# Feed-forward pairs of a two-layer encoder kernel: the fourth weight sum's products one own unit later, its adding transfer in halves, and another adding transfer one own unit sooner

## The chip, the cores and the metric

The kernel runs on one core of a Trainium2 chip. A core has five engines with instruction queues of their own: TensorE (PE: matrix products), VectorE (DVE), ScalarE (ACT), GpSimd (POOL) and SyncE (SP), which in this kernel only starts transfers. PE reads its operands from the on-chip memory and accumulates in a small memory of eight banks. Transfers between the chip's large memory and the on-chip memory are started by SP or by POOL and then run by themselves on the core's 16 DMA engines. The metric is the device time of one execution in microseconds (us), the median of several runs.

## What is computed

A two-layer encoder over 256 rows of 2048 numbers, all float32. Cut to what matters here:

```python
def sq_relu_mlp(h, g, w1, w2):
    a = jax.nn.relu(rms_norm(h, g) @ w1)      # w1: 2048 x 8192
    return (a * a) @ w2                       # w2: 8192 x 2048

h = h + attention_a(h) @ a_w_out              # projections, gated attention
h = h + sq_relu_mlp(h, g0, w1[0], w2[0])      # first feed-forward layer
k_sh, v_sh = split(rms_norm(h) @ kv_w)
h = h + attention_b(h, k_sh, v_sh) @ b_w_out
h = h + sq_relu_mlp(h, g1, w1[1], w2[1])      # second feed-forward layer
```

The change touches the two feed-forward layers alone.

## The kernel before

**Products.** A float32 product is made of three passes. Every block of 128 x 1024 weights is split into a rounded part `hi` (ACT, line 323) and the rest `lo = w - hi` (DVE, line 324); the activations are split likewise. PE then does hi x hi (line 592), hi weights x lo activations (line 594) and lo weights x hi activations (line 596). `hi` and `lo` have three buffers each, so that the splits run at most three blocks ahead of PE, and a split waits until PE has finished with the block three places before.

**Pairs.** The feed-forward weights are worked off in 32 pairs, each two blocks of 512 output columns over all 2048 rows of the sum. 30 of them are "deep": half of a deep pair's work is done by Strassen's scheme, with seven products instead of eight. Its seven weight operands ("forms") are the four quarters `11`, `12`, `21`, `22` and the three weight sums that replace them as the pair goes on, T3 = 22 + 12, then T2 = T3 + 11, then T1 = 12 + 11, then T4 = T2 + 21. There are four sums in all, and the forms of a pair are used in the order 11, T3, T2, T1, and after that 21, T4 and 22. Each form is 128 x 2048, that is two blocks (the second marked h: T4, T4h), with six matmuls of 512 columns per block. The other half of a pair is eight "own units" of plain products, a4 to a7 and b4 to b7, with twelve matmuls each. A pair is thus 14 blocks of forms and 8 own units, 180 matmuls.

**Who makes the sums.** T3 and T2 are made by DVE (line 964), half by half. T1 and T4 are made by an *adding transfer*, started by POOL (line 974): it fetches the other quarter from the large memory and adds it in place, T1 onto the tile of quarter 12, T4 onto the tile of T2 (which is that of T3, `wT3`). An adding transfer can start only when the old content has been read.

**Order.** A plan is written out before any instruction: for every kind of pair a string gives the order of own units (a4, b4, ...) and of forms (F, the next of 21, T4, 22 in the order of the table `FO`). The kinds are `early` (first pair of a layer, not deep), `second` (the next one, deep), `ahead0` and `ahead1` (first weight matrix, later pairs), `deep0` and `deep1` (second weight matrix). After the first two pairs of a layer they alternate deep0, ahead0, deep1, ahead1, three times round, and end with deep0, deep1. The last three own units of a pair (b5, b6, b7) stand between the first four forms of the next. Tables such as `W2S` say how many own units ahead of a pair its quarters 12, 22, 21, 11 are fetched, its T3 is made, and its T1 is started (the sixth number). The splits run along that plan with up to three blocks in hand (`top_up`), and so do the fetches of own units (`raw`, `zraw`). On DVE, ACT, PE and SP the instructions stay in written order; on POOL a scheduler may move them.

**Other work beside it.** The results of the first weight matrix need a squared ReLU and a turn of the tile: DVE transposes into `z` (line 440), and for some of them 16 small transfers move `z` to `q` in one hop (line 466, half of them started by POOL, half by SP); later ACT reads `q` (line 1037, then 1042 and 1044) and DVE finishes (line 1048, sums in lines 395 to 398 and 405). Lines 936 and 299 are SP's fetches of quarters (`w`) and own units (`raw`).

Of the kernel before, what the change touches and what calls it, by code (L numbers as in the profile page):

```python
# [46 lines left out]
    "LONG": ((0, 1, 2, 5, 9, 10, 11, 14, 14), (0, 0, 0, 4, 7, 9), (0, 0, 1, 2, 5, 5), (1, 0, 1, 4, 5, 5)),  # L47
    "OFH": (11, 10, 2, 7, 7, 6),
    "OFK": (9, 9, 4, 8, 8, 4),
# [3 lines left out]
    "OSH": (10, 7, 9, 6, 5, 1),  # L53
    "OSK": (9, 7, 4, 7, 5, 1),
    "OUTH": "F a2 a3 a4 b2 a5 b3 b4 F F G G b5 a6 a7 G b6 b7 G c2 G c3 G d2 c4 c5 c6 G c7 d3 d4",
# [18 lines left out]
    "XOH": (9, 13, 12, 11),  # L74
    "XOK": (10, 14, 12, 14),
    "XS": (0, 5, 5, 0),
# [23 lines left out]
def trunk(ctx: ExitStack, tc: tile.TileContext, xT, xr, gs, hg, bf, wgate, w_in, w_oa, w1a, w1fa, w1sa, w2fa, w2sa,  # L100
# [188 lines left out]
    def load(parts=1, queue=SY, apart=None):  # L289
        src = units.popleft()  # L290
        if isinstance(src, Form):
            raws.append((src, ()))
            return
        extra[1] += 1
        raw = qkv.tile([P, UN], F32, name="zraw", tag="z", bufs=2) if extra[0] and extra[1] % 5 == 0 else wraw.tile([P, UN], F32, name="raw")
        n = UN // parts
        cuts = [slice(i * n, (i + 1) * n) for i in range(parts)]
        if apart is None:
            queue.dma_start(raw, src)
        else:  # L300
            for q, c in zip((queue, apart), cuts):
                q.dma_start(raw[:, c], src[:, c])
        raws.append((raw, cuts))

    def issue(parts=1):
        form = None
        if not raws:
            load(parts)
        raw, cuts = raws.popleft()
        if not cuts:  # L310
            form, half = raw, raw.half
            assert form.name in form.pair.has, "unit early"
            if form.name in ("T3", "T2"):
                assert form.name + str(int(half)) in form.pair.has, "unit early"
            form.pair.issued.add(form.name)
            raw, cuts = form.pair.t[form.name], [slice(0, form.pair.cols - UN if half else UN)]
            if half:
                raw = raw[:, UN:]
        n = cuts[-1].stop
        hi = wsp.tile([P, n], F32R, name="hi" if n == UN else "hih", bufs=3 if n == UN else 1)  # L320
        lo = wsp.tile([P, n], F32R, name="lo" if n == UN else "loh", bufs=3 if n == UN else 1)
        for c in cuts:
            S.activation(hi[:, c], raw[:, c], AF.Copy)  # L323
            V.tensor_tensor(lo[:, c], raw[:, c], hi[:, c].bitcast(F32), op=ALU.subtract)  # L324
        ready.append((hi, lo, n < UN))
        if form and form.pair.deep and form.name == "T3":
            make(form.pair, "T2", int(half))
        elif form and form.pair.order == "second" and form.name == "T2":
            put(form.pair, "T4", int(half))
        elif form and half == form.pair.wide:  # L330
            if form.name == "T3":
                make(form.pair, "T2")
            elif form.name == "T2" and form.pair.adds:
                put(form.pair, "T4")
# [5 lines left out]
    def top_up(ahead=AHEAD, early=EARLY):  # L340
        while (units or raws) and sum(1 for r in ready if not r[2]) <= ahead and not (half_next() and any(r[2] for r in ready)):
            issue()
        while units and sum(1 for r in raws if r[1]) < early + extra[0]:
            load()
# [593 lines left out]
    def make(p, name, half=None):  # L938
        t = p.t
        if half == 1:  # L940
            pass
        elif name == "T3":
            if p.order in ("query", ""):
                t[name] = query_room(0)
            elif p.order == "kv0":
                t[name] = query_room(3)
            elif p.order in LAZY:
                t[name] = acts.tile([P, 2 * UN], F32, name="wT3", tag="act")[:, :UN]
            else:
                t[name] = prob.tile([P, 4 * UN], F32, name="wT3", tag="p", bufs=1) if p.order == "early" else room("bias", "wT3")  # L950
        else:
            t[name] = t[{"T1": "12", "T2": "T3", "T4": "11"}[name]]
        a, b = {"T1": ("12", "11"), "T3": ("22", "12"), "T2": ("T3", "11"), "T4": ("21", "T2")}[name]
        cols = slice(0, p.cols) if half is None else slice(half * UN, min(half * UN + UN, p.cols))
        d, a, b = (t[i][:, cols] for i in (name, a, b))
        if name == "T3":
            assert {"22", "12"} <= p.has and "T1" not in p.has, "T3 order"
        if name == "T1":
            assert "T30" in p.has and "T31" in p.has, ("T1 order", p.order, p.has, p.units, getattr(p, "at", 0))
        for k in (0, 1):  # L960
            if half in (None, k):
                p.has.add(name + str(k))
        p.has.add(name)
        V.tensor_tensor(d, a, b, op=ALU.add)

    def put(p, name, half=None):

        at, other = {"T1": ("12", "11"), "T4": ("T2", "21")}[name]
        p.t[name] = p.t[at]
        if name == "T1":  # L970
            assert "T30" in p.has and "T31" in p.has, ("T1 order", p.order, p.has, p.units, getattr(p, "at", 0))
        p.has.add(name)
        cols = slice(0, p.cols) if half is None else slice(half * UN, half * UN + UN)
        G.dma_start(p.t[name][:, cols], p.big[other][:, cols], accum_op=ALU.add)
# [388 lines left out]
```

## Time and profile before

| what | value |
|---|---|
| device time, median of 3 runs | 2053.66 us (2053.36 to 2055.16) |
| span of the profiled execution, first to last instruction | 2051.8 us |
| PE busy | 2042.6 us, 100% |
| DVE, ACT, POOL busy | 87%, 68%, 12% |
| granted TensorE clock | 1.000 |
| first feed-forward layer | about 366 to 1023 us of the span |
| second feed-forward layer | about 1384 us to the end |

The page gives no time of the profiled execution other than its span; the median of the runs is 1.9 us longer. The rows of the profile read: line, engine, operation, output<-inputs, count, then busy time and mean duration, or, in a view in order of time, the start and the length in us ahead of the instruction. Idle time of the engine just before an instruction stands in square brackets with what ended it.

### The profile page before, as it was taken

What the parts mean: (1) busy time and instruction counts of PE and PEld (TensorE: products, weight loads), DVE (VectorE), ACT (ScalarE), POOL (GpSimd) and SP (SyncE); (2) the same over time, 40 slices, a digit from 0 to 9 for tenths busy, and PEclk for the clock granted to TensorE, in tenths of its full rate; (3) what the DMA queues carried; (4) which work ended last, traced back from release to release, by engine and by line L of the source; (5) the groups of instructions that cost most, each with busy time, mean ns of one, the idle gap of its engine ahead of it and who ended that gap; (6) DMA issues with size and microseconds to landing.
All of it is one profiled execution on the core that took longest, in us unless ns stands there. A gap on an engine that the chain in (4) does not pass through costs nothing.

```text
span 2051.8 us, 27095 instructions
## 1 busy us (share of the span) xinstructions
PE 2042.6 (100%) x9062; PEld 1688.9 (82%) x9062; DVE 1784.1 (87%) x2065; ACT 1404.8 (68%) x1805; POOL 244.2 (12%) x351
## 2 busy tenths in 40 slices
PE   9999999999999999999999999999999999999999
PEld 8888888878888888888878888888888888888887
DVE  7788798899898898899988788889988988988996
ACT  7766676677677676677778666667866676776764
POOL 1121010021111102101012111100111111111020
PEclk9999999999999999999999999999999999999999
DMA  8898888898888898898879888888988888988985
GB/s 321 259 293 273 272 279 245 306 268 266 296 258 285 259 297 271 248 292 273 264 242 300 278 256 285 258 264 286 286 290 267 271 262 289 264 287 261 295 260 149
DMA packets 175021, 557.78 MB, mean 272 GB/s; under 512 B 40592, under 2 KB 69152, under 8 KB 152096
## 3 DMA queue, kind: packets, MB, share of 16 engines
q1 hardware_dynamic: 153824, 464.99, 63.7%
q0 software_dynamic: 20768, 90.75, 22.5%
q8 instruction: 71, 1.16, 0.2%
q14 instruction: 70, 0.57, 0.1%
q10 hardware_dynamic: 288, 0.30, 0.1%
HBM read 516.07 MB, written 27.29 MB: 265 GB/s over the span
## 4 chain that ended last, share of the span: by engine, by line
PE 94%; DVE 3%; DMA 1%; ACT 1%; issue 1%; SPq 0%; ACTq 0%; POOL 0%; DVEq 0%; POOLq 0%
PE acc L596 22%; PE acc L592 22%; PE acc L594 22%; PE s L596 9%; PE s L592 9%; PE s L594 9%; DVE lo L324 1%; DMA raw<-in_w_in 1%; PE po L729 1%; PE po L766 1%; ACT hi L323 0%; PE po L767 0%; PE po L728 0%; DMA turn<-z 0%; DMA raw<-in_w_qb 0%
## 5 line engine op out<-in xcount | busy, mean ns | idle before, releaser
L324 DVE TENSOR_TENSOR lo<-raw,hi 128x1024 fp32r<-128x1024 f32 (+1 forms) x409 | 494.1, 1212 | 80.4 <-ACT hi L323 76.3
L323 ACT ACTIVATE hi<-raw 128x1024 fp32r<-128x1024 f32 (+1 forms) x409 | 429.7, 1054 | 192.2 <-PE acc L594 131.0
L592 PE MATMUL acc<-hi,act 128*128 128x512 f32 x1774 | 496.2, 392 | 1.2 <-ACT hi L323 1.1
L596 PE MATMUL acc<-lo,act 128*128 128x512 f32 x1774 | 491.1, 390 | 1.5 <-DVE lo L324 1.4
L594 PE MATMUL acc<-hi,act 128*128 128x512 f32 x1774 | 490.3, 389 | 0.0
L596 PEld LDWEIGHTS acc<-lo,act 128*128 128x128 f32 x1774 | 332.3, 188 | 73.2 <-DVE lo L324 4.2
L594 PEld LDWEIGHTS acc<-hi,act 128*128 128x128 f32 x1774 | 332.9, 188 | 69.7
L592 PEld LDWEIGHTS acc<-hi,act 128*128 128x128 f32 x1774 | 331.4, 188 | 69.8 <-ACT hi L323 1.9
L323 ACT ACTIVATE hi<-w 128x1024 fp32r<-128x1024 f32 x254 | 267.1, 1058 | 127.9 <-PE acc L594 85.2
L324 DVE TENSOR_TENSOR lo<-wT,hi 128x1024 fp32r<-128x1024 f32 x220 | 267.1, 1221 | 65.0 <-ACT hi L323 61.4
L324 DVE TENSOR_TENSOR lo<-w,hi 128x1024 fp32r<-128x1024 f32 x254 | 305.5, 1218 | 15.3 <-ACT hi L323 13.5
L323 ACT ACTIVATE hi<-wT 128x1024 fp32r<-128x1024 f32 x220 | 232.0, 1060 | 97.3 <-PE acc L594 46.2
L592 PE MATMUL s<-hi,act 128*128 128x512 f32 x530 | 146.3, 391 | 0.2 <-ACT hi L323 0.2
L596 PE MATMUL s<-lo,act 128*128 128x512 f32 x530 | 145.2, 389 | 0.4 <-DVE lo L324 0.3
L594 PE MATMUL s<-hi,act 128*128 128x512 f32 x530 | 144.8, 388 | 0.0
L466 POOL DMA_DIRECT2D q<-z x192 | 95.6, 511 | 251.8 <-DVE z L440 217.3
L596 PEld LDWEIGHTS s<-lo,act 128*128 128x128 f32 x530 | 99.0, 188 | 22.0 <-DVE lo L324 1.7
L594 PEld LDWEIGHTS s<-hi,act 128*128 128x128 f32 x530 | 99.3, 188 | 20.7
L592 PEld LDWEIGHTS s<-hi,act 128*128 128x128 f32 x530 | 98.9, 188 | 20.9 <-ACT hi L323 0.8
L596 PE MATMUL s<-lo,S 128*128 128x512 f32 x288 | 88.8, 389 | 0.7 <-DVE lo L324 0.7
L592 PE MATMUL s<-hi,S 128*128 128x512 f32 x288 | 89.4, 392 | 0.0
L594 PE MATMUL s<-hi,S 128*128 128x512 f32 x288 | 88.7, 389 | 0.0
(217 smaller groups left out, 2285.6 us busy)
## 6 DMA issues: line engine op xcount, KB each, us to landing
raw<-in_w_in SPq DMA_DIRECT2D x75, 512.0 KB, 5.8
w<-in_w2fa SPq DMA_DIRECT2D x32, 1024.0 KB, 6.5
w<-in_w2fb SPq DMA_DIRECT2D x32, 1024.0 KB, 6.0
w<-in_w1fa SPq DMA_DIRECT2D x28, 1024.0 KB, 6.9
w<-in_w1fb SPq DMA_DIRECT2D x28, 1024.0 KB, 7.6
raw<-in_w2sa SPq DMA_DIRECT2D x52, 512.0 KB, 7.4
raw<-in_w2sb SPq DMA_DIRECT2D x50, 512.0 KB, 6.8
raw<-in_w_kv SPq DMA_DIRECT2D x48, 512.0 KB, 5.1
```

The source lines that it names most:

```text
L323: S.activation(hi[:, c], raw[:, c], AF.Copy)
L324: V.tensor_tensor(lo[:, c], raw[:, c], hi[:, c].bitcast(F32), op=ALU.subtract)
L466: (G if i % 2 else SY).dma_start(dst[32 * j : 32 * j + 32, i * n : (i + 1) * n], z[32 * i : 32 * i + 32, j * n : (j + 1) * n])
L592: TE.matmul(ps[:, cols], xh, cut(hi, j), start=first, stop=False, **kw)
L594: TE.matmul(ps[:, cols], xl, cut(hi, j), start=False, stop=False, **kw)
L596: TE.matmul(ps[:, cols], xh, cut(lo, j), start=False, stop=last, **kw)
L729: TE.matmul(s[:, P : 3 * P], q[:, a, P:T], k[:, a], start=True, stop=True)
L766: TE.matmul(po[:, :T], v[:, 0, a * P : (a + 1) * P], pT[:, :2], start=True, stop=False)
```

## The change

Three things are changed, all in feed-forward pairs.

1. In the pairs `second`, `ahead0`, `ahead1` and `deep0` the form T4 is used one own unit later: after a5 instead of before it (in `deep0` after b4). In `second` and `ahead` pairs form 22 stays where it was; `deep1` is as before.
2. The adding transfer that makes T4 is started in two halves in every deep pair: each as soon as that half of T2 has been split. Before, only `second` did so; the other 28 deep pairs started one transfer of 1 MB after the second half of T2.
3. For the second of every two pairs of the second weight matrix (`W2S`, and `W2L` for the last one), the adding transfer of T1 is started two own units ahead of the pair instead of one.

```diff
-    "ORD": {"second": "a4 F F a5 a6 a7 F b4", "ahead1": "a4 F F a5 a6 a7 F b4", "ahead0": "F a4 F a5 a6 a7 F b4", "deep1": "a4 F b4 F a5 F a6 a7",
+    "ORD": {"second": "a4 F a5 F a6 a7 F b4", "ahead1": "a4 F a5 F a6 a7 F b4", "ahead0": "F a4 a5 F a6 a7 F b4", "deep1": "a4 F b4 F a5 F a6 a7",
...
-        "deep0": "a4 F F F b4 a5 a6 a7"},
+        "deep0": "a4 F F b4 F a5 a6 a7"},
...
-    "W2L": (6, 5, 5, 5, 3, 1),
-    "W2S": (7, 7, 4, 5, 3, 1),
+    "W2L": (6, 5, 5, 5, 3, 2),
+    "W2S": (7, 7, 4, 5, 3, 2),
...
         if form and form.pair.deep and form.name == "T3":
             make(form.pair, "T2", int(half))
-        elif form and form.pair.order == "second" and form.name == "T2":
+        elif form and form.pair.deep and form.name == "T2":
             put(form.pair, "T4", int(half))
```

What this moves, at three places. First DVE in the pair `second` of the first feed-forward layer, where form 21 ends; `wT3_3799` holds T4, `raw_3861` is own unit a5, `w21` is form 21, and the last row (line 964) makes the first half of the *next* pair's T3. Before:

```order
L324 TENSOR_TENSOR lo_4057<-w21_3753,hi_4056 128x1024
L1016 TENSOR_TENSOR s_3866<-s_3865,p7_3940 128x512
L324 TENSOR_TENSOR lo_4078<-wT3_3799,hi_4077 128x1024
L324 TENSOR_TENSOR lo_4088<-wT3_3799,hi_4087 128x1024
L405 TENSOR_TENSOR Sh_4033<-sum_4034,Sh_4033 128x512
L405 TENSOR_TENSOR Sh_4033<-sum_4035,Sh_4033 128x512
L324 TENSOR_TENSOR lo_4102<-raw_3861,hi_4101 128x1024
L324 TENSOR_TENSOR lo_4114<-zraw_3921,hi_4113 128x1024
L324 TENSOR_TENSOR lo_4126<-raw_3964,hi_4125 128x1024
L964 TENSOR_TENSOR wT3_4145<-w22_4073,w12_4003 128x1024
```

And now:

```order
L324 TENSOR_TENSOR lo_4057<-w21_3753,hi_4056 128x1024
L1016 TENSOR_TENSOR s_3866<-s_3865,p7_3940 128x512
L324 TENSOR_TENSOR lo_4078<-raw_3861,hi_4077 128x1024
L324 TENSOR_TENSOR lo_4090<-wT3_3799,hi_4089 128x1024
L405 TENSOR_TENSOR Sh_4033<-sum_4034,Sh_4033 128x512
L405 TENSOR_TENSOR Sh_4033<-sum_4035,Sh_4033 128x512
L324 TENSOR_TENSOR lo_4104<-wT3_3799,hi_4103 128x1024
L964 TENSOR_TENSOR wT3_4119<-w22_4073,w12_4003 128x1024
L324 TENSOR_TENSOR lo_4122<-zraw_3921,hi_4121 128x1024
L324 TENSOR_TENSOR lo_4134<-raw_3964,hi_4133 128x1024
```

The split of a5 takes the place that T4's first block had, and the next pair's T3 stands ahead of the splits of a6 and a7 instead of behind them. In `ahead1` and in the `deep0` pairs that an `ahead0` follows, T3 moves ahead of the same number of splits or more.

Second, POOL from pair `deep0` on: `w12_4330` and `wT3_4527` are T1 and T4 of the first `ahead0` pair, the hop of eight is that pair's `z`, and `w12_4671` is T1 of the `deep1` pair after it, whose T4 ends the piece. Before:

```order
L974 DMA w12_4330<-in_w1fa 128x2048
L974 DMA wT3_4527<-in_w1fa 128x2048
L466 DMA q_4857<-z_4856 32x256 x8
L974 DMA w12_4671<-in_w2fa 128x2048
L974 DMA wT3_4838<-in_w2fa 128x2048
```

And now:

```order
L974 DMA w12_4331<-in_w1fa 128x2048
L974 DMA wT3_4499<-in_w1fa 128x1024 x2
L466 DMA q_4859<-z_4858 32x256 x3
L974 DMA w12_4673<-in_w2fa 128x2048
L466 DMA q_4859<-z_4858 32x256 x5
L974 DMA wT3_4840<-in_w2fa 128x1024 x2
```

T4 is two transfers, and T1 of the `deep1` pair now stands in the midst of the hop. This holds in all six `ahead0` pairs.

Third, SP in the same `ahead0` pair; `raw` and `zraw` are its own units a7 to b7 and, from `in_w2sa`, the first of the next pair; `w22`, `w11`, `w21` are quarters of the next pair. Before:

```order
L936 DMA w22_4673<-in_w2fa 128x2048
L299 DMA raw_4679<-in_w1sa 128x1024
L299 DMA raw_4741<-in_w1sa 128x1024
L936 DMA w11_4776<-in_w2fa 128x2048
L299 DMA raw_4782<-in_w1sa 128x1024
L299 DMA zraw_4794<-in_w1sa 128x1024
L299 DMA raw_4806<-in_w1sa 128x1024
L936 DMA w21_4820<-in_w2fa 128x2048
L299 DMA raw_4865<-in_w2sa 128x1024
L466 DMA q_4857<-z_4856 32x256 x8
```

And now:

```order
L936 DMA w22_4675<-in_w2fa 128x2048
L299 DMA raw_4681<-in_w1sa 128x1024
L299 DMA raw_4743<-in_w1sa 128x1024
L299 DMA raw_4755<-in_w1sa 128x1024
L936 DMA w11_4780<-in_w2fa 128x2048
L936 DMA w21_4798<-in_w2fa 128x2048
L299 DMA zraw_4804<-in_w1sa 128x1024
L299 DMA raw_4816<-in_w1sa 128x1024
L299 DMA raw_4868<-in_w2sa 128x1024
L466 DMA q_4859<-z_4858 32x256 x8
```

The fetch of quarter 21 now stands ahead of the fetches of b6 and b7. Elsewhere SP's order is as before.

## The prediction

> **What bounds the kernel now.** I read the page's busy times and its chain first, then PE's busy time stage by stage, then PE in order of time where a stage loses any.
>
> ```profile
> PE 2042.6 (100%) x9062; PEld 1688.9 (82%) x9062; DVE 1784.1 (87%) x2065; ACT 1404.8 (68%) x1805; POOL 244.2 (12%) x351
> PE 94%; DVE 3%; DMA 1%; ACT 1%; issue 1%; SPq 0%; ACTq 0%; POOL 0%; DVEq 0%; POOLq 0%
> ```
>
> PE is busy all the time and holds 94% of the chain that ended last. Busy is not full speed, so I look by stage: the pair `second` of each layer (420 to 455, 1437 to 1472), and the pairs after it.
>
> ```profile
> 420.00:455.00 35.00, 33.57 (x147) 27.13 (x147) 32.81 (x40) 26.81 (x29) 5.84 (x10) 1.00 0.93 269
> 455.00:1003.00 548.00, 548.00 (x2416) 452.97 (x2415) 495.11 (x486) 378.62 (x400) 63.85 (x107) 1.00 0.88 274
> 1437.00:1472.00 35.00, 34.93 (x153) 28.29 (x152) 34.06 (x40) 27.68 (x31) 6.18 (x11) 1.00 0.93 282
> 1472.00:2040.00 568.00, 568.00 (x2505) 469.81 (x2504) 507.12 (x496) 387.62 (x403) 63.81 (x107) 1.00 0.86 268
> ```
>
> In the two long stretches PE runs 2416 matmuls in 548 us and 2505 in 568 us: 0.2268 us each in both. Three starts show that this is full speed: the own unit b6 of an `ahead0` pair, two form blocks, and b7; twelve matmuls each time take 2.72 us, 0.2267 each.
>
> ```profile
> 541.46 1.07 PE L592 MATMUL s<-hi,act 128*128 128x512 f32 x4
> ...
> 544.18 0.62 PE L592 MATMUL acc<-hi,Sh 128*128 128x512 f32 x2
> ...
> 546.90 1.07 PE L592 MATMUL s<-hi,act 128*128 128x512 f32 x4
> ```
>
> 2416 x 0.2267 is 547.7 and 2505 x 0.2267 is 567.9, so both stretches together lose some 0.4 us. Here 28 of the 30 deep pairs lie, where most of the change is: nothing is to be won there. The Trainium skill's page "Perfetto Trace Analysis" (Identifying the Most-Contended Engine) says that matmul busy time misleads and that the busy share of weight loads tells the distance from the limit. Its 82% would leave room; the trace disagrees, as the same share (453 of 548, 83%) stands in a stretch at full pace.
>
> `second` does lose time, at form 21's second block and at T4:
>
> ```profile
> 431.83 0.61 PE L594 MATMUL acc<-hi,act 128*128 128x512 f32 x2
> 433.80 0.72 PE L596 MATMUL acc<-lo,act 128*128 128x512 f32 x2 [1.35 <-DVE lo L324]
> 434.36 0.63 PE L592 MATMUL acc<-hi,act 128*128 128x512 f32 x2
> 435.53 0.74 PE L596 MATMUL acc<-lo,act 128*128 128x512 f32 x2
> 436.11 0.62 PE L592 MATMUL acc<-hi,act 128*128 128x512 f32 x2
> ...
> 1451.23 0.64 PE L592 MATMUL acc<-hi,act 128*128 128x512 f32 x2
> 1452.96 0.62 PE L592 MATMUL acc<-hi,act 128*128 128x512 f32 x2
> ```
>
> A form block is six matmuls, 1.36 us. T4's first block takes 436.11 - 434.36 = 1.75 us in the first layer and 1.73 in the second: 0.39 and 0.37 lost, 0.76 together. Block 21h loses 1.5 at 433.80 in the first layer (1.97 us where two matmuls take 0.45). What DVE does then:
>
> ```profile
> 432.53 1.22 DVE L324 TENSOR_TENSOR lo<-w,hi 128x1024 fp32r<-128x1024 f32 x1
> 433.66 0.69 DVE L1016 TENSOR_TENSOR s<-s,p 128x512 f32<-128x512 f32 x1
> 434.26 2.35 DVE L324 TENSOR_TENSOR lo<-wT,hi 128x1024 fp32r<-128x1024 f32 x2
> 436.53 1.28 DVE L405 TENSOR_TENSOR Sh<-sum,Sh 128x512 fp32r<-128x512 f32 x2
> 437.74 1.22 DVE L324 TENSOR_TENSOR lo<-raw,hi 128x1024 fp32r<-128x1024 f32 x1
> 438.87 1.22 DVE L324 TENSOR_TENSOR lo<-zraw,hi 128x1024 fp32r<-128x1024 f32 x1
> 441.14 1.22 DVE L964 TENSOR_TENSOR wT<-w,w 128x1024 f32<-128x1024 f32 x1
> ```
>
> It works without a pause, one split each 1.13 us (437.74 to 438.87). T4's first `lo` ends at about 435.45, and PE starts the `lo` pass at 435.53: DVE is late here.
>
> **T4 one own unit later, in `second`.** Now a5's split stands in that place on DVE. Its `lo` still ends at 435.45, 1.1 after PE's start there (434.36); an own unit wants it only after eight matmuls, 1.81, not after four, 0.91. The wait goes: -0.76 in the two layers. Next late could be T4h or a6. Going on in the new order with the rows' pitches (1.13 a split or sum, 1.2 for the two of line 405): T4's `lo` ends 2.3 after that start and is wanted at 3.6; T4h's at 4.7, wanted at 5.0; the next pair's T3 ends at 5.9, a6's `lo` at 7.0, wanted at 7.25. Margins of 0.2 to 0.3, thin but above nothing. Wrong by half a microsecond, each gives up to 0.3 back per layer; so this part lies between -0.8 and +0.6, and I take -0.7, since the pitches are rows of the same stretch. Block 21h's wait stands ahead of everything that moves, and I leave it.
>
> **T4 later, in the other pairs.** PE waits for nothing there; the cover is the three blocks in hand. ACT does wait for T4's arrival (us, times, the longest):
>
> ```profile
> ACT hi L323 <- DMA wT<-in_w1fa: 6.5, 5, 2.6
> ```
>
> The longest, 2.6, is less than the 2.72 us of an own unit, so these waits go; worth 0 to PE, which doesn't feel them. What it costs: the next pair's T3 moves forward on DVE, in `deep0` to just behind T4h's split, and it needs quarter 22, fetched by SP. In one `deep0`, with PE's start on T4 (where b4 will now start):
>
> ```profile
> 638.93 0.99 SPq L936 DMA_DIRECT2D w<-in_w1fa  x2
> ...
> 642.12 0.62 PE L592 MATMUL acc<-hi,act 128*128 128x512 f32 x2
> ...
> 649.40 1.22 DVE L964 TENSOR_TENSOR wT<-w,w 128x1024 f32<-128x1024 f32 x1
> DMA to landing us min/median/max: 4.7/6.7/10.2
> ```
>
> T4h's buffer comes free at 642.12; a `hi` (1.06) and a `lo` (1.22) on, T3 could start at 644.4 instead of 649.40. The fetch of 22 starts at 638.93: 5.5 us for what takes 4.7 at least and 6.7 in the middle, so DVE may wait 1 us. a5's `lo`, next behind, ends two pitches after T3's start, at 646.7 without a wait, and is wanted 5.44 + 1.81 after 642.12, at 649.4. Cover 2.7: at the median I take 0, at the slowest it costs 10.2 - 5.5 - 2.7 = 2.0 a place, at six places.
>
> **Halves.** 28 more transfers on POOL, 0.9 us each, 25 us beside 244 busy of 2052: hidden by POOL's idle time. Landing, first of the halves in `second`, then of all adding transfers of this layer:
>
> ```profile
> DMA to landing us min/median/max: 9.9/10.8/11.7
> DMA to landing us min/median/max: 7.8/9.9/12.9
> ```
>
> The second half starts when the whole did and lands at worst 11.7 - 7.8 = 3.9 us later, at best sooner, as half is ahead of it; against 2.72 us more of time. I take 0. The Trainium skill's page "DMA: Bandwidth & Descriptors" (Anatomy of one DMA) speaks against halves: each transfer has some 2.0 us of fixed cost. By it the second half would come at most 2 us later, the sum would stay -0.7, and the hop behind it is what could suffer; no run here shows the fixed cost alone.
>
> **T1 sooner, and SP's order.** T1 had been started after the hop of `ahead0`, now it goes in after three of eight, so five hop transfers queue behind 1 MB. Rows of the hop and T1 (534.51), ACT's first use of the hop (543.73) and its next split, then an `ahead1`, where T1 already leads the hop:
>
> ```profile
> 529.22 3.97 POOL L466 DMA_DIRECT2D q<-z  x8 [23.75 <-DVE z L440]
> 534.51 0.93 POOL L974 DMA_DIRECT2D w<-in_w2fa  x1 [1.32 <-DMA q<-z]
> ...
> 543.73 1.05 ACT L1037 ACTIVATE q<-q 128x1024 f32<-128x1024 f32 x1
> 544.68 1.04 ACT L323 ACTIVATE hi<-raw 128x1024 fp32r<-128x1024 f32 x1
> ...
> 608.41 0.86 POOL L974 DMA_DIRECT2D w<-in_w2fa  x1 [20.95 <-DVE wT L964]
> 610.84 3.49 POOL L466 DMA_DIRECT2D q<-z  x7 [1.56 <-DVE z L440]
> DMA to landing us min/median/max: 8.3/8.3/8.3
> DMA to landing us min/median/max: 2.8/5.5/6.4
> ```
>
> There T1 lands at 616.7 and the hop's first at 610.84 + 6.4 = 617.2: in order behind it, the rest within 2 us. In `ahead0` T1 would start behind three hop transfers of 0.5, at about 530.8, and land at 539.1 by that row, 543.7 by the slowest of the layer; the hop's rest 1.5 us on, 540.6 to 545.2, against 543.73. The split after it starts at 544.68, and PE wants that block at 546.9 (b7's start above): 1.17 us of cover behind its 1.05. So 0 by the nearest row, and at most 0.3 by the slowest, times six places: 1.8. On SP the fetches of b6 and b7 now stand behind that of quarter 21, which can't start before its room is free (526.78):
>
> ```profile
> 526.78 0.33 SPq L936 DMA_DIRECT2D w<-in_w2fa  x1
> 538.03 1.06 ACT L323 ACTIVATE hi<-zraw 128x1024 fp32r<-128x1024 f32 x1 [1.21 <-PE s L594]
> ```
>
> b6 is split at 538.03; fetched from 527.2 it lands by 537.4 even if it takes the 10.2 us of the slowest quarter. Cost 0, but it puts 1 MB more traffic beside T1 just then, which is why I keep the slowest landing as an end.
>
> **Sum.** -0.7 in `second`, 0 elsewhere: span 2051.8 - 0.7 = 2051.1. The median of the runs is 1.9 above the span, so 2053.66 - 0.7 = 2053.0. A change of 0.2%, 4.1 us, is what a measurement of this kernel tells from none.
>
> **Rivals.** (1) The wait only moves: T4h and a6 in `second` take it over as above, +0.6 at most: 2053.7 to 2054.3. For it: margins of 0.2. (2) Slower: the hop of `ahead0` comes late behind T1. Its place is ACT at line 1037, in six pairs. It begins to cost when T1 takes over 12.6 us (530.8 + 12.6 + 1.5 = 543.73 + 1.17), and decides when it takes 13.4: 0.8 us lost six times, 4.8 less 0.7. At 14.5 it is 1.9 x 6 - 0.7 = 10.7: 2064.4. Against it: 8.3 and a maximum of 12.9. (3) T3 of `deep0` and `ahead1` waits for quarter 22: at 10.2 us 2.0 x 6 - 0.7, 2065; against it the median, 6.7. (4) Faster: 21h's wait goes too, if DVE comes there earlier: -0.7 - 1.5, 2051.4; nothing on DVE ahead of it moves. More than 4.1 us isn't there to be won.
>
> **Chances.** The forecast 0.58; (1) 0.20; (2) 0.12, two thirds of it past 4.1 us; (3) 0.06, two thirds likewise; (4) 0.04. Slower by over 0.2%: 0.08 + 0.04 and 0.02 for what I don't see, 0.14; faster 0.02; within 0.84. The range goes from all of `second`'s waits gone (2051.4, less 0.2 for the runs' own spread) to (2) and (3) at less than 4.1 us: 2051.2 to 2057.0.
>
> **What would show it.** Right: in `second` T4's first block lasts 1.36 us, 21h still waits in the first layer, and PE's two long stretches keep 0.2267 us a matmul. ACT's waits for `wT` from `in_w1fa` shrink. Wrong: idle time of ACT at line 1037 that a hop ends, DVE's line 964 waiting for a quarter, or a wait at a6 or T4h of `second`.

## The result, and the profile after

The changed kernel takes 2061.2 us, the median of six runs (2058.6 to 2065.7); the kernel before took 2055.75, the median of six too, the three shown ahead among them (2053.4 to 2057.4). Beside the experiments below its median was 2055.9 to 2056.4, so the 2053.66 from which the forecast started lay some 2 us low. The ratio is 1.0024, with a 95% interval of 1.0014 to 1.0034: slower by 0.24%, some 5 us. The forecast was 2053.0, with a range that ended at 2057.0.

The profiled execution has a span of 2059.8 us, 8.0 more than that of before. Runs of one kernel lie up to 10 us apart here, so single places are read from the traces, and what an edit is worth from the medians. The page of the changed kernel, busy times and the chain that ended last:

```profile
PE 2046.7 (99%) x9062; PEld 1686.7 (82%) x9062; DVE 1784.0 (87%) x2065; ACT 1408.2 (68%) x1805; POOL 271.5 (13%) x379
PE 88%; DMA 6%; DVE 3%; ACT 1%; issue 1%; SPq 1%; ACTq 0%; DVEq 0%; POOLq 0%
```

PE's share of the chain fell from 94% to 88%, and transfers hold 6% of it instead of 1%. POOL has 28 instructions and 27 us more, as the halves were costed. PE's busy time by stage:

```profile
420.00:455.00 35.00, 33.63 (x147) 26.98 (x146) 32.77 (x40) 26.72 (x29) 5.76 (x10) 1.00 0.95 283
455.00:1003.00 548.00, 547.74 (x2408) 450.88 (x2407) 492.87 (x483) 378.10 (x398) 76.80 (x121) 1.00 0.89 273
1437.00:1475.00 38.00, 35.30 (x152) 27.80 (x151) 33.11 (x39) 26.92 (x30) 7.26 (x12) 1.00 0.88 254
1475.00:2046.00 571.00, 570.33 (x2507) 469.32 (x2506) 508.97 (x497) 390.62 (x405) 76.70 (x121) 1.00 0.87 268
```

The first long stretch holds 2408 matmuls where it held 2416, 8 x 0.2267 = 1.8 us. The second layer's `second` needs 38 us for 152 matmuls (35 for 153 before), and the last stretch 571 us for 2507, that is 2.7 us above 0.2267 each (0.1 before). For the place of it I add up, from the starts of PE's matmuls, what each pair takes beyond 0.2267 us a matmul:

| us lost by PE | before | after |
|---|---|---|
| layer 1: `second` and first `deep0` | 2.6 | 3.4 |
| layer 1: three `ahead0` and the pairs behind them | 0.0 | 0.9 |
| layer 2: `early` (in front of all that is moved in this layer) | 0.0 | 1.2 |
| layer 2: `second` and first `deep0` | 0.9 | 5.5 |
| layer 2: three `ahead0` and the pairs behind them | 0.0 | 1.4 |

That is 8.9 more; the rest of the execution came out 0.9 shorter. Of what the change moves, two kinds of place lose. The first is the `ahead0` pair. ACT and PE in order of time, at the rows that stood at 543.73 and 546.90 before:

```profile
543.15 1.05 ACT L323 ACTIVATE hi<-wT 128x1024 fp32r<-128x1024 f32 x1
545.35 1.06 ACT L1037 ACTIVATE q<-q 128x1024 f32<-128x1024 f32 x1 [1.14 <-DMA q<-z]
546.32 1.04 ACT L323 ACTIVATE hi<-raw 128x1024 fp32r<-128x1024 f32 x1
...
545.91 0.61 PE L592 MATMUL acc<-hi,Sh 128*128 128x512 f32 x2
547.41 1.19 PE L592 MATMUL s<-hi,act 128*128 128x512 f32 x4
550.51 0.69 PE L592 MATMUL acc<-hi,Sh 128*128 128x512 f32 x2
```

ACT waits 1.14 us for the hop, b7's split behind it ends at 547.36, and PE starts b7 at 547.41. The block before b7 lasts 1.50 us instead of 1.36, and from b7's start to the next block's it is 3.10 instead of 2.72. All six `ahead0` pairs have such a wait at line 1037: 1.14, 0.45, 0.84, 0.65, 1.21 and 1.22 us. The second kind is DVE in `second`; here the second layer:

```profile
1455.49 2.36 DVE L324 TENSOR_TENSOR lo<-wT,hi 128x1024 fp32r<-128x1024 f32 x2
1460.42 1.23 DVE L964 TENSOR_TENSOR wT<-w,w 128x1024 f32<-128x1024 f32 x1 [2.57 <-issue]
1461.56 2.35 DVE L324 TENSOR_TENSOR lo<-raw,hi 128x1024 fp32r<-128x1024 f32 x2
...
1457.21 0.62 PE L592 MATMUL acc<-hi,act 128*128 128x512 f32 x2
1458.57 0.62 PE L592 MATMUL acc<-hi,act 128*128 128x512 f32 x2
1462.84 1.19 PE L596 MATMUL acc<-lo,act 128*128 128x512 f32 x4 [0.93 <-DVE lo L324]
1472.05 1.21 PE L596 MATMUL s<-lo,act 128*128 128x512 f32 x4 [0.76 <-DVE lo L324]
```

T4's first block lasts 1458.57 - 1457.21 = 1.36 us: its wait is gone, as forecast. But DVE stands still for 2.57 us ahead of the next pair's T3. That T3 needs quarter 22, which was started at 1454.51 and landed at 1460.34, 0.08 ahead of it. a6's split is queued behind T3, and PE loses 1.2 us at a6 and 1.05 at b4.

### The profile page after: what moved, and what is told of

Read it like the earlier page. It is cut to its first block, busy times and chain, and to the rows that moved or that the text cites. A ratio compares the mean times of both kernels' runs of the same rounds, so it can differ in the third digit from the quotient of the medians.

```text
span 2059.8 us, 27140 instructions
## 1 busy us (share of the span) xinstructions
PE 2046.7 (99%) x9062; PEld 1686.7 (82%) x9062; DVE 1784.0 (87%) x2065; ACT 1408.2 (68%) x1805; POOL 271.5 (13%) x379
## 4 chain that ended last, share of the span: by engine, by line
PE 88%; DMA 6%; DVE 3%; ACT 1%; issue 1%; SPq 1%; ACTq 0%; DVEq 0%; POOLq 0%
PE acc L596 20%; PE acc L592 20%; PE acc L594 20%; PE s L596 8%; PE s L592 8%; PE s L594 8%; DVE lo L324 1%; DMA q<-turn 1%; DMA raw<-in_w2sb 1%; DMA q<-z 1%; PE po L729 1%; PE po L766 1%; ACT hi L323 1%; DMA w<-in_w1fb 1%; DMA w<-in_w2fa 0%
```

## The experiments

Four theories stood against each other. **H**: the hop of `ahead0` comes late. **Q**: T3 was moved ahead of its quarter 22. **D**, formed after the first four runs: from `second` to the first `deep0` DVE works without pause, so a wait taken from T4 comes back further on. **V**: a part is only a difference between executions of any kernel. Times and ratios to the kernel before, run beside each:

| kernel | median us (runs) | ratio, 95% interval |
|---|---|---|
| `only_t1` | 2056.64 (11) | 1.0002 [0.9992, 1.0012] |
| `only_order` | 2059.93 (11) | 1.0010 [1.0000, 1.0021] |
| `only_halves` | 2055.52 (11) | 0.9997 [0.9987, 1.0007] |
| `order_halves` | 2058.01 (11) | 1.0007 [0.9997, 1.0016] |
| `ahead0_and_t1` | 2058.62 (11) | 1.0016 [1.0007, 1.0024] |
| `after_old_ahead0` | 2055.45 (11) | 1.0001 [0.9992, 1.0010] |
| `after_21_later` | 2057.18 (11) | 1.0006 [0.9997, 1.0015] |
| `order_22_sooner` | 2061.34 (8) | 1.0024 [1.0013, 1.0034] |
| `order_sums_pool` | 2075.13 (5) | 1.0096 [1.0082, 1.0110] |
| `order_lighter_dve` | 2064.40 (4) | 1.0036 [1.0022, 1.0050] |
| `second_only` | 2057.40 (10) | 1.0003 [0.9994, 1.0012] |
| `deep0_only` | 2057.83 (10) | 1.0005 [0.9996, 1.0015] |
| `second_drop` | 2054.36 (10) | 0.9991 [0.9982, 1.0001] |

### The three edits one by one

`only_t1` has the two numbers of `W2S` and `W2L`; `only_halves` the line of `issue`; `only_order` the four strings; `order_halves` strings and line, that is the changed kernel without T1.

> The kernel before with the third edit alone: T1 of the second-matrix pairs is started two own units ahead, so that in the six ahead0 pairs it stands behind three of the hop's eight transfers on POOL. Theory H (the hop comes late behind T1; ACT at line 1037 waits for it, and PE loses at b7 and at the first forms of the next pair): 2 to 4 us longer than before, with idle time of ACT ahead of line 1037 in all six ahead0 pairs. Theory Q (the loss is DVE's T3, line 964, waiting for quarter 22, brought by the new order): no change, within 0.5 us. Theory V (the loss in the second layer's first pairs is a difference between executions of any kernel): no change in the median.

> The kernel before with the second edit alone: T4's adding transfer in two halves in every deep pair. Theories H, Q and V: no change, within 0.5 us, since T4 isn't waited for by PE in those pairs. Rival (more transfers on POOL's queue delay the hops behind them): 0.5 to 2 us longer, with idle time of ACT ahead of line 1037.

> The kernel before with the first edit alone: T4 one own unit later in second, ahead0, ahead1 and deep0; transfers of T4 whole, T1 as before. Theory H: the hop is untouched, so 0.5 to 0.8 us shorter than before, by the waits at T4 in the two second pairs. Theory Q: DVE's T3 waits for quarter 22 and holds the splits behind it, so 1 to 4 us longer, with PE losses at a5, a6 and b4 of second and deep0 pairs. Theory V: as H, the first pairs of the second layer changing by some 2 us from one execution to the next.

> The changed kernel without its third edit: T1 started one own unit ahead, as before. Theory H: the loss at the hop goes, so 0.7 us shorter than the kernel before, or the same where the first pairs of the second layer vary; 3 to 5 us shorter than the changed kernel. Theory Q: the loss stays, 2 to 4 us longer than the kernel before. If the two act together, it lies between.

The halves cost nothing that the time shows. T1 alone doesn't either, against theory H as it then stood. The order alone costs 2 us by its ratio, with an interval that ends at zero (by the medians 3.6), and `order_halves` 1.4. So none of the three carries the 5 us alone. What tells is how far the hop's two halves land ahead of the moment at which ACT comes to line 1037, in the six `ahead0` pairs, and how long T1 takes to land:

| kernel | POOL's half ahead by, us | SP's half ahead by | T1 to landing | PE loss, six places |
|---|---|---|---|---|
| before | 6.2 to 7.5 | 5.8 to 7.1 | 8.7 to 11.5 | 0 |
| `only_t1` | 1.5 to 2.5 | 2.0 to 2.7 | 8.6 to 10.1 | 0 |
| `only_order` | 4.5 to 5.2 | -1.3 to 1.3 | 8.3 to 9.8 | 1.3 |
| `order_halves` | 4.7 to 5.1 | -1.2 to 0.4 | 8.2 to 9.6 | 1.2 |
| `ahead0_and_t1` | -1.1 to -0.1 | -1.5 to -0.3 | 11.4 to 12.3 | 3.9 |
| after | -0.8 to -0.2 | -1.1 to -0.2 | 11.1 to 12.3 | 2.3 |
| `after_old_ahead0` | 1.3 to 2.3 | 1.7 to 2.3 | 9.5 to 10.4 | 0 |
| `after_21_later` | 1.2 to 2.2 | 1.8 to 2.4 | 9.1 to 10.5 | 0 |

T1 takes 4 to 5 us of the hop's lead, the order 6 to 7 us of the lead of SP's half. T1 alone leaves 1.5 us or more; the order alone leaves 1.3 at most and is late in some pairs, where nearly all of its 1.3 us is lost in one; with both the hop is late in all six. Theory H was restated so, and tried from both ends.

### The hop: both causes, and each taken away

`ahead0_and_t1` is the kernel before with only these lines (of the line `ORD` only the entry of `ahead0` is shown):

```diff
-"ahead0": "F a4 F a5 a6 a7 F b4"
+"ahead0": "F a4 a5 F a6 a7 F b4"
-    "W2L": (6, 5, 5, 5, 3, 1),
-    "W2S": (7, 7, 4, 5, 3, 1),
+    "W2L": (6, 5, 5, 5, 3, 2),
+    "W2S": (7, 7, 4, 5, 3, 2),
```

> The kernel before with two parts alone: the new order in ahead0 pairs (with SP's fetch of quarter 21 ahead of b6 and b7) and T1 two own units ahead. Second, ahead1 and deep0 pairs and T4's transfers are as before. Theory H in its present form (each of the two takes 2 to 5 us of the 6 to 7 us by which the hop lands ahead of ACT's line 1037, and only both together make it late): ACT idle 0.4 to 1.2 us ahead of line 1037 in all six ahead0 pairs, PE's losses at T2h, b7 and T1 there 2 to 4 us in all, and the time longer by that. If T1 alone or the order alone had done it, it would show with T1 alone, where no ahead0 pair lost any. Theory Q: no change, as DVE's T3 of deep0 and ahead0 is not moved.

1.0016: 3.3 us longer, by medians 2.2, and 3.9 us of PE's time at the six places. `after_old_ahead0` is the changed kernel with the first of these lines undone.

> The changed kernel with the old order in ahead0 pairs; everything else is kept. Theory H: the hop lands 1.5 us or more ahead of ACT's line 1037 in ahead0 pairs, as with T1 alone, and PE loses nothing at their b7 and the forms behind it: 2 to 3 us shorter than the changed kernel, some 2 us longer than the kernel before. The losses of theory Q (a6 and b4 of the second layer's second, a5 or a6 of the first deep0) and of theory D (11h and T3h of the first deep0) stay.

1.0001: as fast as the kernel before, 4.7 us under the changed one by the two ratios. The 2 us above the kernel before that were expected don't show in the time; the trace loses 1.7 us more than before at the places of theories Q and D. The loss at the six `ahead0` pairs is zero. So the string of `ahead0` beside the earlier T1 makes the slowdown. A string moves the form T4, splits, and fetches; `after_21_later` takes only a fetch back (and keeps all else of the change):

```diff
-    "W2S": (7, 7, 4, 5, 3, 2),
+    "W2S": (7, 7, 3, 5, 3, 2),
```

> The changed kernel with one number undone in its effect: in W2S the third number, 4 to 3, so that SP's fetch of quarter 21 stands behind b6 and b7 again in ahead0 pairs, as in the kernel before. The order of forms, T4's halves and T1's earlier start stay. Theory H, in this form: it is SP's fetch of quarter 21 ahead of b6 and b7 that holds SP's half of the hop back (its last transfer starts some 3 us later), and T1 that holds POOL's; without the first the hop lands 1 to 2.5 us ahead of ACT's line 1037, PE loses nothing at b7, and the time is that of the kernel before within 2 us, as with the old order in ahead0. Rival (it is the place of the form itself, by what DVE and ACT split and when): the losses at b7 stay, 5 us longer than before.

1.0006, 3.7 us under the changed kernel by the two ratios, and again no loss at the six places. In the traces the two kernels' instructions stand in the same order on PE, DVE, ACT and POOL; on SP only the six fetches of quarter 21 stand elsewhere. So beside the earlier T1 it is SP's order that makes the hop late, not the form's place. How much it costs is known less well: 3.3 to 4.7 us by ratios that are each good to 2 us, 2.3 and 3.9 us by PE's losses in the two traces that have it. SP in order of time in the first `ahead0` pair, first before (b6, b7; then, behind the row at 526.78 that the prediction shows, the hop), then after (quarters 11 and 21, b6, b7, the next pair's first own unit, the hop):

```profile
514.00 0.43 SPq L299 DMA_DIRECT2D zraw<-in_w1sa  x1
520.44 0.33 SPq L299 DMA_DIRECT2D raw<-in_w1sa  x1
...
528.95 5.05 SPq L466 DMA_DIRECT2D q<-z  x8
```

```profile
514.38 13.10 SPq L936 DMA_DIRECT2D w<-in_w2fa  x2
527.52 0.43 SPq L299 DMA_DIRECT2D zraw<-in_w1sa  x1
528.00 0.43 SPq L299 DMA_DIRECT2D raw<-in_w1sa  x1
528.53 0.59 SPq L299 DMA_DIRECT2D raw<-in_w2sa  x1
529.31 8.86 SPq L466 DMA_DIRECT2D q<-z  x8
```

SP waits for quarter 21's room in the changed kernel from 514.8 to 527.15, with the fetches of b6 and b7 behind it. Then 1 MB and three times 0.5 MB start within 1.4 us, right ahead of the hop: 2.5 MB, where before it was quarter 21 and one own unit, 1.5 MB. What SP waited for while it started the hop's eight, and how the hop's transfers landed (all 16; 3.3 to 4.9 us before), in the changed kernel:

```profile
SPq L466 <- DMA raw<-in_w2sa: 2.1, 1, 2.1
SPq L466 <- DMA raw<-in_w1sa: 1.1, 1, 1.1
SPq L466 <- DMA zraw<-in_w1sa: 0.8, 1, 0.8
DMA to landing us min/median/max: 6.0/11.4/12.7
```

The last three of the eight wait for the landing of three fetches that stand eight places ahead of them. POOL's side, where T1 (531.12) now leads five of the hop:

```profile
529.58 1.54 POOL L466 DMA_DIRECT2D q<-z  x3 [23.76 <-DVE z L440]
531.12 0.98 POOL L974 DMA_DIRECT2D w<-in_w2fa  x1
531.72 2.40 POOL L466 DMA_DIRECT2D q<-z  x4
535.96 0.50 POOL L466 DMA_DIRECT2D q<-z  x1 [1.84 <-DMA q<-z]
DMA to landing us min/median/max: 12.3/12.3/12.3
```

The last line is T1's own landing. Beside SP's 2.5 MB it takes 12.3 us; with SP's old order it took 9.7 in the same place (`only_t1`). Over the six pairs it is 11.1 to 12.3 in the changed kernel and 9.1 to 10.5 in `after_21_later`.

### T3 and quarter 22

> The kernel before with the new order in deep0 pairs alone. Theory Q: T3 of the next pair waits for quarter 22 by 0 to 1.6 us in the deep0 pairs, but the blocks in hand cover it except in the first deep0 of each layer, where a6 or a5 loses 0.4 us; 0.8 us longer in all, which the time can't tell from no change. Theory D: nothing at 11h and T3h beyond what they lose before (0 and 0.22). Theory H: nothing at the ahead0 pairs.

> The kernel before with the new order in the pair second of each layer alone. Theory D: T4's waits go (0.38 and 0.36), and come back at 11h and T3h of the first deep0 (0.3 and 0.1 in the first layer, 0.5 and 0.1 in the second). Theory Q: in the second layer T3 waits for quarter 22 by 0 to 2.5 us, and a6 and b4 lose 0.4 to 2 us together. Nothing at the ahead0 pairs. In all 0 to 2 us longer than before; by the prediction's own sum it would be 0.7 us shorter.

`deep0_only` and `second_only` have one string each. In `deep0_only` the first `deep0` loses 0.40 at a6 in the first layer (0.23 at a4 goes) and 0.40 at a5 in the second, as expected. In `second_only` the second layer's T3 waits only 0.19 us for quarter 22, and nothing is lost at a6. That wait was 2.57 us in the changed kernel, 2.12 in `only_order`, 0.66 in `order_halves`: it depends on when that execution's quarter lands, and with it PE's loss at a6 and b4 (2.3, 1.8 and 0.4 us). The two kernels without the loss at the hop fit in: T3 waits 0.81 and 0.90 us, and PE loses 0.5 and 0.6. Theory Q is thus a price of 0.8 us in the two first `deep0` and of 0 to 2.3 in the second layer's `second`. Neither kernel's time can be told from the one before.

Both profiles have another loss that no theory named: 1.5 and 1.1 us at b7 of an `ahead0` pair, where T1 landed 11.3 and 12.5 us after its start and ACT waited 2.3 and 1.9 us for it. An earlier start of T1 might help there, which no run shows; the prediction gave that edit no gain at all.

`order_22_sooner` is `only_order` with

```diff
-    "W1F": (7, 5, 1, 5, 4, 3),
-    "W2F": (6, 5, 1, 5, 4, 3),
+    "W1F": (7, 6, 1, 5, 4, 3),
+    "W2F": (6, 6, 1, 5, 4, 3),
```

> The kernel before with the first edit (T4 one own unit later in four kinds of pair), and quarter 22 of deep0 and ahead0 pairs fetched one own unit sooner (second number of W1F and W2F, 5 to 6). Theory Q (DVE's T3, line 964, was moved ahead of its quarter and holds the splits behind it): the idle time of DVE ahead of line 964 goes, and with it PE's losses at a6 and b4 of the second layer's pair second (1.8 us with the first edit alone) and at a6 or a5 of the first deep0 (0.4 a layer); about 2 us shorter than the first edit alone. Theory D (DVE works without pause from the pair second to the first deep0, so that what PE no longer waits at T4 it waits at form 11): the losses at 11h and T3h of the first deep0, 0.6 to 0.85 a layer, stay. Rival: the hop of eight transfers, which SP now starts behind quarter 22, comes late, and ACT waits at line 1037 in second and deep0 pairs; then no gain.

The rival came true. DVE no longer waits at T3, though PE still loses 0.9 us at b4 of the second layer's `second`, where DVE waited 1.14 us for ACT's split of T4h. And the quarter now stands ahead of another hop on SP, and ACT waits for that one (first `deep0` of the second layer; SP, then ACT):

```profile
1494.51 9.09 SPq L466 DMA_DIRECT2D q<-z  x8
...
1505.47 1.06 ACT L1037 ACTIVATE q<-q 128x1024 f32<-128x1024 f32 x1 [2.45 <-DMA q<-z]
```

1.0024: the wait was moved, from 2 us at T3 to 2.9 us at T4h and a5 of that pair.

### DVE's work between `second` and the first `deep0`

> The kernel before with the first edit, and the two subtractions of line 405 (0.64 us each on DVE, two per use, two uses a pair of the first matrix) given to POOL: DVE has 1.3 us less to do twice between the pair second and the first deep0. Theory D: the waits at 11h and T3h of the first deep0 (0.7 and 0.85 us with the first edit alone) fall below 0.3 a layer, since DVE comes there 1.3 to 2.6 us sooner, and T4's wait stays away. Rival (the wait at 11h is not DVE's amount of work but one late transfer): 11h and T3h stay as they are. The waits for quarter 22 are untouched, or longer by what DVE comes sooner.

`order_sums_pool` changes `V` to `G` in line 405 for the feed-forward sums. It is 19 us slower and says little on theory D, since PE comes to 11h late. DVE, then POOL, in `second` of the first layer:

```profile
434.85 3.89 DVE L324 TENSOR_TENSOR lo<-raw,hi 128x1024 fp32r<-128x1024 f32 x1
...
435.13 2.52 POOL L405 TENSOR_TENSOR Sh<-sum,Sh 128x512 fp32r<-128x512 f32 x2
```

A split of 1.22 us takes 3.89 while POOL subtracts: 2.67 more for POOL's 2.52. The work was not taken from DVE, it was made DVE's wait, and in six later pairs T4's transfer starts only as POOL's subtraction ends.

> The kernel before with the first edit, and with the subtraction of line 405 left out: ACT copies the sum in its place, so that the low parts of Sh are not those of the reference. DVE has 1.3 us less to do, twice between the pair second and the first deep0, and POOL nothing more. Theory D (DVE's work without pause sets the pace there): the waits at 11h and T3h of the first deep0 go, 0.7 us in the first layer and 0.85 in the second, and T4's stay away, so that the first edit then does save what it takes from T4. Rival (a late transfer or ACT is what 11h waits for): they stay or grow, as ACT has 1.1 us more.

`order_lighter_dve` writes `S.activation(lo[i], w[i], AF.Copy)` in the place of that subtraction. PE's waits for DVE at T3h go, and in the first layer that at 11h, but ACT's two copies stand ahead of b5's split (ACT, then PE at b5):

```profile
453.50 1.14 ACT L405 ACTIVATE Sh<-sum 128x512 fp32r<-128x512 f32 x2
454.54 1.04 ACT L323 ACTIVATE hi<-raw 128x1024 fp32r<-128x1024 f32 x1
...
455.63 1.19 PE L592 MATMUL s<-hi,act 128*128 128x512 f32 x4 [0.78 <-ACT hi L323]
```

So it couldn't tell. `second_drop` has the string of `second` alone, leaves the subtraction out, and gives no engine other work:

```diff
-            V.tensor_tensor(lo[i], w[i], hi[i].bitcast(F32), op=ALU.subtract)
+            light or V.tensor_tensor(lo[i], w[i], hi[i].bitcast(F32), op=ALU.subtract)
...
-                Sh[c].extend(r[:, i : i + n] for i, n in ((0, UN), (UN, UN), (2 * UN, UN), (3 * UN, UN)))
+                Sh[c].extend(r[:, i : i + n] for i, n in ((0, UN), (0, UN), (2 * UN, UN), (2 * UN, UN)))
```

> The kernel before with the new order in the pair second alone, and with the two subtractions of line 405 left out in both layers: the low parts of Sh are taken to be the high parts, so the products with them are not those of the reference; no engine gets other work for it. DVE has 1.3 us less to do, twice between the pair second and the first deep0. Theory D (DVE's work without pause sets the pace there): PE's waits at 11h and T3h of the first deep0 (0.24 and 0.36 us with the order of second alone, 0.39 and 0.33 in the second layer) fall to below 0.1 each, T4's stay away, and the pair second and the first deep0 of the first layer together lose 0.6 us less than in the kernel before, 2.0 instead of 2.6. Rival (the waits at 11h and T3h have another cause): they stay at 0.6 to 0.7 a layer. Theory Q: DVE, coming sooner, waits longer for quarter 22 ahead of line 964 in the second layer, 0.5 to 3 us, and a6 or b4 may lose by it.

PE's loss in `second` and the first `deep0` together, first and second layer: 2.6 and 0.9 before, 2.9 and 1.2 in `second_only`, 1.6 and 0.6 here. In the first layer only 21h's wait of 1.62 is left. The same blocks on PE, the last two passes of 11h and the start of b5, in the changed kernel and here:

```profile
452.06 0.61 PE L594 MATMUL acc<-hi,act 128*128 128x512 f32 x2
452.69 0.73 PE L596 MATMUL acc<-lo,act 128*128 128x512 f32 x2
453.27 1.10 PE L592 MATMUL s<-hi,act 128*128 128x512 f32 x4
```

```profile
452.11 0.62 PE L594 MATMUL acc<-hi,act 128*128 128x512 f32 x2
452.56 0.62 PE L596 MATMUL acc<-lo,act 128*128 128x512 f32 x2
453.02 1.07 PE L592 MATMUL s<-hi,act 128*128 128x512 f32 x4
```

The `lo` pass comes 0.63 us after the `hi` pass in the one, 0.45 in the other. In the second layer 0.30 stays at 11h, and there DVE had waited 1.32 us for quarter 22. So theory D holds in the first layer by the traces (the time, 0.9991, can't tell it from no change): T4's 0.38 is saved only where DVE has room further on.

**What stays open.** The 1.2 us of `early`, and 1.4 us at T1h, a4 and 21h of `second` behind it, in the profile of the changed kernel. ACT waited there for transfers (a hop, own units), ahead of everything that the change moves in that layer. The same pair lost between 0 (before) and 3.8 us (`ahead0_and_t1`) in the first layer of the profiles, where no edit stands ahead of it. I take them for differences between executions (theory V); what makes them was not tried.

## Where the prediction was right and where it failed

**T4 one own unit later, in `second`** (-0.7). The wait at T4 went in both layers and T4h and a6 took over 0.2 at most in the first, as worked out. What failed is where the working ended. It followed DVE as far as a6 and called the rest gained. DVE had no pause further on either, and the wait came back at 11h and T3h of the next pair: with this string alone 0.24 and 0.36 in the first layer, 0.39 and 0.33 in the second. The term measured +0.2 to +0.3 us a layer, not -0.35. That is rival (1) at a place it didn't name.

**T4 later, in the other pairs** (0). In the first `deep0` of each layer 0.4 is lost at a6 or a5, where T3 waited for quarter 22: the cover of 2.7 us, worked out in a later `deep0`, is smaller there. The quarter for the T3 behind `second` was not looked at. It left at 1450.33 and landed 2.59 us ahead of T3 before, and the move took that lead: 0 to 2.3 us lost. Rival (3) came true at places that it didn't name, and smaller than priced. The 0 also left out a gain. In profiles without the new order PE loses at T4 of one or two `ahead1` pairs where T4's transfer takes 10.9 us or more (8.6 and 9.9 in two of them before): 1.0 and 0.6 us in `only_t1`, 0.3 in `only_halves`, 0.7 in `ahead0_and_t1`, none in the kernel before. With the new order none is lost there.

**Halves** (0). Right by the time: 0.9997. ACT's waits for `wT` from `in_w1fa` are gone, but that is mostly the order's doing: 6.5 us before, 5.9 with the halves alone, 2.0 with the order alone, none with both.

**T1 sooner, and SP's order** (0). This is the step that failed, by 3 to 5 us by the times. First, SP's move was charged to b6 alone. It put 2.5 MB instead of 1.5 right ahead of SP's half of the hop, and that half lost 6 us of its lead; the prediction noted the traffic and did not count the eight transfers queued behind. Second, T1's landing was taken from an `ahead1` pair, 8.3 us, though T1 took 8.7 to 11.5 in the `ahead0` pairs before. It was 8.6 to 10.1 with this edit alone, but 11.1 to 12.3 with SP's transfers beside it. So the 0 rested on a hop that lands at 540.6, and it landed at 544.93 on POOL's side and 545.24 on SP's. The bound did hold: 12.3 is under the 12.9 of the slowest, the hop landed by its 545.2, and the 1.5 us from T1's landing to the hop's last was right (544.93 - 543.44). Third, that bound was priced too low, at 0.3 us a place, since the cover of 1.17 us between ACT and b7 wasn't there in full: a wait of 1.14 us for the hop cost 0.14 ahead of b7 and 0.38 from its start to the next block's. Rival (2) had the place and the mechanism, with T1 alone as its cause; at that it would not have come true, and T1 stayed below the 12.6 us from which it was to cost. That its price at 0.8 us a place, 4.8, is near the 3.3 to 4.7 that the times gave is luck: PE's own loss was 0.7 us a place at most in the changed kernel.

**The rest.** PE at full speed in the long stretches before, 21h's wait untouched in the first layer, no gain in the time beyond `second`: right. The range ended at 2057.0, as rivals (2) and (3) were held under 4.1 us each. Of the 8.2 us between the forecast and the result 2.1 are the low start at 2053.66; with the six runs' 2055.75 in its place the range would have ended at 2059.1, still under 2061.2.

## What to carry to other kernels

Two edits that each leave a little of the same lead must be added up before either is called free: here one took up to 5 us and the other 6 of the 7 by which a hop arrived early, and alone the one could not be told from no change and the other hardly. When a fetch moves on a queue, count everything behind it on that queue, above all small transfers that someone waits for, and not only the fetch that was moved. And where an engine works without pause, follow its queue until it pauses: a wait taken away in front of that comes back behind.

## What the runs showed of the hardware

- On SP and on POOL every transfer of this kernel started only when the one eight places ahead on that queue had landed: SP's sixth, seventh and eighth of the hop started at 533.39, 535.03 and 537.67, each 0.02 us after the landing of such a fetch. The landings of a queue are told by eight semaphores, used in turn, and in the trace these starts wait on the semaphore that will tell of their own landing, so it may be the program's counting; no run tries another. Large fetches ahead of small transfers thus hold back their start too, not only their landing.
- A transfer on POOL's queue is slowed by those on SP's: T1 landed after 9.7 us with 1.5 MB started on SP just ahead of it, and after 12.3 with 2.5 MB. The Trainium skill's page "DMA: Bandwidth & Descriptors" (Issuing engines are not separate DMA queues) says that transfers run on the same 16 engines and interleave whichever engine started them; the trace agrees.
- DVE's split stood still for about as long as POOL's two subtractions ran, 3.89 us instead of 1.22. The Trainium skill's page "SBUF — State Buffer" (SBUF: two separate sides) says that an instruction of DVE with two inputs in that memory and one of GpSimd that reads it exclude each other for the whole instruction; the trace agrees, with 2.67 us of delay beside POOL's 2.52.
